# Differential attention's last product with v stationary and two query blocks moving, z_a with channels on the partitions, and the channel sums by a row of ones

## The chip, the cores and the metric

One NeuronCore of a Trainium2 chip runs the whole layer. The metric is the device time of one execution in microseconds (us); lower is better. Engines are named as the profile names them: PE is TensorE, which multiplies matrices (PEld its weight loads), DVE is VectorE, ACT is ScalarE, POOL is GpSimd, and SP is SyncE, which here issues nearly all DMAs (SPq is its queue).

## The reference

One decoder layer on 1024 tokens of width 1024, all in fp32, with two token mixers beside each other:

```
h = RMSNorm(x)
[q | k | v | z_a | xBC | z_s | dt | gate_logits] = h @ w_in
branch A: 8 heads, two softmax maps of head dimension 64 per head, causal:
    a   = softmax(q0 k0^T) - lam * softmax(q1 k1^T)
    o   = a @ v                                  (v has 128 channels per head)
    y_a = rms_norm(o, subln_w) * (1 - lambda_init) * silu(z_a)
branch B: Mamba-2 SSD (32 heads, chunks of 128, state 128) with a causal
    convolution, gated by silu(z_s) and group-normalised -> y_s
merged = sigmoid(g_a) * (y_a @ w_proj_attn) + sigmoid(g_s) * (y_s @ w_proj_ssd)
out    = x + merged @ w_out
```

The change is in branch A: in `a @ v`, in the norm over the 128 channels of a head behind it, and in the projection of z_a.

## The kernel before

The program has no loops on the chip. A planner (class `Plan`) runs while the program is built: every piece of work is a Python generator, and the planner keeps a time `pl.t` for PE and one for each other engine, adds a cost for each instruction, and lets a piece go on when the planned time of what it needs has come. The order in which the instructions are written down is the order of each engine's queue; on the chip each engine follows its queue and waits on semaphores. So the costs in `mm`, `act`, `tt`, `stt` and `load` change no instruction, only the order. Every matmul is recorded on the line of `mm` (L208), every PE transpose on L217, ACT's work on L234, DVE's on L242 or L250, DMAs on L263.

Precision: most products are made of three matmuls of type fp32r (a high and a low part of each operand, `steps3`): `pma<-w,hH` twice and `pma<-w,hL` once per 128 channels of the contraction. Products with plain fp32 operands (`av`, `pO`, `pc`, `pD`, `pacum`, `nwb`) stand in the trace as two MATMUL records each. A name like `pma<-w,hH` reads: output, moving operand, stationary operand.

The stages, in the order of PE's queue:

- The front (the string `FRONT_ORDER`): `y` and `z` steps make z_s, `e` and `g` make part of the gates, `c` the convolved channels of xBC in pairs of blocks, `d` is dt. Chunks of branch B (names `px`, `pS`, `pO`, `pD`, `ab`, `xdt`) run in the gaps from the front on; `PACE` and `SLOW` are the planned distances between them.
- Attention, head by head (`att_proj`): for each of 8 token blocks t, PE multiplies h by the 512 columns of q, k, v and z_a of one head into one PSUM bank `pma`. `att_evac` takes the bank apart: squares for the norm of q and k, a copy of v, `tanh` of the z_a part and (tanh+1)*z_a into `zg` (tokens on the partitions). `qk_stack` transposes q and k (`pq`). `att_block` makes one query block of 128 tokens: scores (`sc`, two maps), exponentials with row sums, the difference of the two maps in `p` (not yet divided by the first map's row sum), then transposes of p in groups of up to four 128x128 blocks (`pa`, copied to `at` by ACT), and then the last product: for each key block j one matmul with at's block stationary and v's block moving, 128 columns wide, into `av` (query tokens on the partitions, channels along the row). Behind it ACT squares `av` with a row sum, POOL makes `f` = (sum + e1)^-0.5 (`rsqrt`, two instructions; e1 holds the epsilon scaled by the softmax's sum), DVE makes y = av * f * zg, PE transposes y (`pya`), ACT copies it to `yt` scaled by subln_w, and four blocks together are stored to `ya_d`.
- The other gates (`pg`), while the last head ends.
- `products`: y_s @ w_proj_ssd and y_a @ w_proj_attn, then `final`: the product with w_out. Sums of w_out's blocks for this are made beforehand by POOL (`weight_sums(2, ...)`, tile `os`), started 11 us after the end of attention's projections in planned time.

PSUM has eight banks, all from one ring (`trs`).

Of the kernel before, what the change touches and what calls it, by code (L numbers as in the profile page):

```python
# [8 lines left out]
F32 = mybir.dt.float32  # L9
# [6 lines left out]
P = 128  # L16
# [129 lines left out]
def tile_hybrid_layer(ctx: ExitStack, tc: tile.TileContext, x, norm_w, w_in, q_norm_w, k_norm_w,  # L146
# [22 lines left out]
    cv_d = dram.tile([3072, S], F32, name="cv_d")  # L169
    z_d = dram.tile([GROUPS, S, 512], F32, name="z_d")  # L170
# [10 lines left out]
    qkm, atm, ytm, smids = Share(mids, 4), Share(mids, 4), Share(mids, 2), Share(mids, 10)  # L181
# [25 lines left out]
    def mm(o, lhsT, rhs, start, stop, after=0.0, **kw):  # L207
        nc.tensor.matmul(o, lhsT=lhsT, rhs=rhs, start=start, stop=stop, **kw)  # L208
# [24 lines left out]
    def act(o, i, f, after, **kw):  # L233
# [5 lines left out]
        return pl.op("A", c, after)  # L239

    def tt(o, a, b, op, after, eng="V"):
# [5 lines left out]
        return pl.op("V", 0.07 + 0.07 * sb + 1.042e-3 * n, after, sb)  # L247

    def stt(o, a, s, b, op0, op1, after):
        nc.vector.scalar_tensor_tensor(out=o, in0=a, scalar=s, in1=b, op0=op0, op1=op1)  # L250
        sb = not in_ps(a, b)
        return pl.op("V", 0.07 + 0.07 * sb + 1.042e-3 * o.free_size() + (0.0 if isinstance(s, float) else 0.06), after, sb)
# [8 lines left out]

    def load(o, i, after=0.0):
        nc.sync.dma_start(out=o, in_=i)  # L263
# [15 lines left out]
    nc.gpsimd.memset(mhalf, -0.5)  # L279
    mone = const.tile([P, 1], F32, name="mone")  # L280
# [511 lines left out]
    def att_proj(h):  # L792
# [5 lines left out]
        zg = bigt([P, NT, P], name=f"zg{h}")  # L798
# [34 lines left out]
    def att_evac(h, t, pm, k, qn, cell):  # L833
        v, zg = hd[h][0:2]
        at = pe_done()
        t2 = act(qn, pm[:, 0:256], AF.Square, at)
        t1 = act(zg[:, t, :], pm[:, 384:512], AF.Tanh, at, scale=0.5)
# [62 lines left out]
    def att_block(h, qb, pk, q):  # L900
# [46 lines left out]
        rec, n0, cc, e1 = tin(1, "rec"), tin(1, "n0"), tin(1, "cc"), tin(1, "e1")  # L947
# [3 lines left out]
        t_e = act(e1, sums[0], AF.Square, at, scale=(P * EPS) ** 0.5)  # L951
# [9 lines left out]
        ats = []  # L961
        for j in range(0, qb + 1, 4):
            w = min(4, qb + 1 - j)
            km = yield from pl.get(atm)
            k = yield from pl.get(trs)
            pt = trt(f"pa{h}{qb}{j}")
            for i in range(w):
                tp(pt[:, i * P:(i + 1) * P], pr[0][:, (j + i) * P:(j + i + 1) * P])
            cell = [midt(name=f"at{h}{qb}{j}"), km]
            pl.spawn(at_evac(pt, k, w, cell), pe_done())  # L970
            ats.append(cell)
        bigs.give(pk[0], pl.t + 0.1)
        for c in ats[:1]:
            while len(c) < 3:
                yield pl.t + 0.1
            yield c[2]
        k = yield from pl.get(trs)
        av = trt(f"av{h}{qb}")
        for j in range(qb + 1):
            c = ats[j // 4]  # L980
# [18 lines left out]
        trs.give(k, at)  # L999
        lefts[h][0] -= 1  # L1000
        if lefts[h][0] == 0:
            for i in ks:
                heads.give(i, at)
        yield at
# [1224 lines left out]
```

## Time and profile before

| | |
|---|---|
| median of 3 runs | 1582.83 us (1580.4 to 1583.64) |
| the profiled execution's own time | 1580.41 us |
| its span in the profile | 1578.7 us |
| mean granted TensorE clock | 0.998 |
| PE, PEld busy share | 98%, 82% |
| DVE, ACT, POOL busy share | 75%, 60%, 50% |
| DMA queue q1, share of 16 engines | 55.7% |

The profile's page has one execution. "Busy" for PE counts from a matmul's start to its modelled end, and neighbouring matmuls overlap, so PE's 98% says that it hardly ever stands without work, and not how long one matmul holds it; that is read from the distance between starts. The stage limits used below are read from the first and last start of the stages' tiles: the front ends and attention begins at 581 us (first `pma`), the last `pya` is at 1275 us, and the rest is products and the final product, to 1579 us.

### The profile page before, as it was taken

What the parts mean: (1) busy time and instruction counts of PE and PEld (TensorE: products, weight loads), DVE (VectorE), ACT (ScalarE), POOL (GpSimd) and SP (SyncE); (2) the same over time, 40 slices, a digit from 0 to 9 for tenths busy, and PEclk for the clock granted to TensorE, in tenths of its full rate; (3) what the DMA queues carried; (4) which work ended last, traced back from release to release, by engine and by line L of the source; (5) the groups of instructions that cost most, each with busy time, mean ns of one, the idle gap of its engine ahead of it and who ended that gap; (6) DMA issues with size and microseconds to landing.
All of it is one profiled execution on the core that took longest, in us unless ns stands there. A gap on an engine that the chain in (4) does not pass through costs nothing.

```text
span 1578.7 us, 24834 instructions
## 1 busy us (share of the span) xinstructions
PE 1553.7 (98%) x7858; PEld 1299.0 (82%) x7858; DVE 1183.6 (75%) x2143; ACT 939.4 (60%) x2273; POOL 785.3 (50%) x906
## 2 busy tenths in 40 slices
PE   7999999999999999999999999999999999999999
PEld 5777888888888888888888888888888888888887
DVE  6778867568787778767778787877556687898985
ACT  7653434467565576778677777776666554443350
POOL 3274465345555554546574846454756745332005
PEclk9999999999999999999999999999999999999999
DMA  6576698744454552424373522333336697798846
GB/s 227 162 250 194 230 301 284 247 153 139 133 150 157 151 158 96 134 62 122 111 236 122 152 89 81 110 112 118 107 134 224 193 366 253 267 323 273 302 140 220
DMA packets 254821, 287.38 MB, mean 182 GB/s; under 512 B 18391, under 2 KB 162528, under 8 KB 254690
## 3 DMA queue, kind: packets, MB, share of 16 engines
q1 hardware_dynamic: 254686, 285.79, 55.7%
q8 instruction: 62, 1.02, 0.3%
q14 instruction: 69, 0.57, 0.1%
q10 hardware_dynamic: 4, 0.00, 0.0%
HBM read 196.47 MB, written 89.26 MB: 181 GB/s over the span
## 4 chain that ended last, share of the span: by engine, by line
PE 85%; ACT 3%; DVE 3%; DMA 3%; POOL 3%; issue 2%; SPq 0%; POOLq 0%; DVEq 0%; ACTq 0%
PE pma L208 19%; PE pz L208 11%; PE py L208 5%; PE fYc L208 5%; PE sc L208 4%; PE pO L208 4%; PE av L208 4%; PE fXc L208 3%; PE fZc L208 3%; PE px L208 3%; PE fYg L208 3%; PE pg L208 2%; PE pmz L208 2%; PE pa L217 2%; PE poz L208 1%
## 5 line engine op out<-in xcount | busy, mean ns | idle before, releaser
L208 PE MATMUL pma<-w,hH 128*128 128x512 f32 x1024 | 343.8, 404 | 0.0
L208 PEld LDWEIGHTS pma<-w,hH 128*128 128x128 f32 x1024 | 187.7, 189 | 32.9 <-DVE xdt L242 0.2
L208 PE MATMUL pma<-w,hL 128*128 128x512 f32 x512 | 205.7, 402 | 0.0
L234 ACT ACTIVATE w<-raw 128x512 fp32r<-128x512 f32 (+1 forms) x166 | 101.3, 629 | 56.0 <-DMA raw<-wf_d 21.7
L242 DVE TENSOR_TENSOR w<-raw,w 128x512 fp32r<-128x512 f32 (+1 forms) x134 | 107.1, 817 | 27.0 <-ACT w L234 24.1
L234 ACT ACTIVATE p<-p,nm 128x256 f32<-128x256 f32 (+7 forms) x128 | 98.8, 774 | 33.8 <-DVE nm L916 33.3
L208 PEld LDWEIGHTS pma<-w,hL 128*128 128x128 f32 x512 | 96.5, 188 | 16.6
L242 POOL TENSOR_TENSOR rawf<-rawf,rawf 128x512 f32<-128x512 f32 x54 | 71.8, 1330 | 75.1 <-DVE wp L242 30.5
L208 PE MATMUL fYc<-ft,wp 128*128 128x512 f32 x432 | 106.5, 392 | 2.4 <-DVE ft L242 1.8
L208 PEld LDWEIGHTS fYc<-ft,wp 128*128 128x128 f32 x432 | 80.3, 188 | 20.2 <-DVE ft L242 2.2
L208 PE MATMUL pz<-w,ft 128*128 128x512 f32 x384 | 90.1, 391 | 0.9 <-DVE w L242 0.9
L234 ACT ACTIVATE wp<-rawp 128x512 fp32r<-128x512 f32 x72 | 44.1, 627 | 78.4 <-POOL rawp L242 25.6
L242 POOL TENSOR_TENSOR os<-os,os 128x512 f32<-128x512 f32 x48 | 66.9, 1393 | 36.4 <-DMA os<-in_w_in_dram 14.8
L208 PEld LDWEIGHTS pz<-w,ft 128*128 128x128 f32 x384 | 71.7, 188 | 16.0 <-DVE w L242 1.3
L242 POOL TENSOR_TENSOR rawp<-rawp,rawp 128x512 f32<-128x512 f32 x36 | 54.4, 1521 | 54.2 <-DVE wp L242 50.2
L234 ACT ACTIVATE ab<-ab,nac 128x128 f32<-128x128 f32 x256 | 78.5, 397 | 3.5 <-POOL ab L1482 3.4
L916 DVE CUSTOM_DVE_ANT_0 p<-sc,maskb 128x512 f32<-128x512 f32 (+3 forms) x128 | 72.4, 584 | 6.6 <-PE sc L208 6.0
L274 POOL TENSOR_TENSOR rs<-rs,mhalf 128x4 f32<-128x4 f32 (+1 forms) x71 | 72.8, 1025 | 5.9
L208 PE MATMUL av<-v,at 128*128 128x128 f32 x576 | 75.2, 275 | 0.0
L208 PEld LDWEIGHTS av<-v,at 128*128 128x128 f32 x576 | 72.5, 191 | 3.2
L234 ACT ACTIVATE wp<-rawf 128x512 fp32r<-128x512 f32 x100 | 60.5, 624 | 17.5 <-POOL rawf L242 16.3
L948 POOL TENSOR_TENSOR rec<-s,mone 128x1 f32<-128x1 f32 x64 | 37.2, 583 | 63.7 <-ACT p L234 62.5
(376 smaller groups left out, 4410.3 us busy)
## 6 DMA issues: line engine op xcount, KB each, us to landing
raw<-in_w_in_dram SPq DMA_DIRECT2D x104, 256.0 KB, 3.2
rawf<-in_w_in_dram SPq DMA_DIRECT2D x72, 256.0 KB, 4.7
ab<-act_d SPq DMA_DIRECT2D x32, 512.0 KB, 4.7
wf_d<-os SPq DMA_DIRECT2D x48, 256.0 KB, 5.1
cv_d<-cv SPq DMA_DIRECT2D x48, 256.0 KB, 2.9
raw<-wf_d SPq DMA_DIRECT2D x48, 256.0 KB, 3.3
t_d<-ts SPq DMA_DIRECT2D x24, 512.0 KB, 4.0
os<-in_w_in_dram SPq DMA_DIRECT2D x32, 256.0 KB, 3.8
```

Source lines behind the costliest of these rows:

```text
L208: nc.tensor.matmul(o, lhsT=lhsT, rhs=rhs, start=start, stop=stop, **kw)
L217: nc.tensor.transpose(out=o, in_=i, identity=ident if idn is None else idn)
L234: nc.scalar.activation(o, i, f, **kw)
L242: (nc.vector if eng == "V" else nc.gpsimd).tensor_tensor(out=o, in0=a, in1=b, op=op)
L274: nc.gpsimd.tensor_tensor(out=dst, in0=dst, in1=mhalf[:, 0:cols], op=ALU.pow)
L916: nc.vector.tensor_tensor_reduce(out=p[:, j:e], in0=sc[i][:, 0:e - j], in1=maskb[:, S - n + j:S - n + e], scale=-1.0, scalar=nms[i - 1] if ...
L948: nc.gpsimd.tensor_tensor(out=rec, in0=sums[1], in1=mone, op=ALU.pow)
```

## The change

The last product is turned. Query blocks are taken in pairs (`att_pair`): p of both blocks is transposed, with the transposes laid out so that for each key block the two query blocks stand side by side in `at` (256 columns). v's block is now the stationary operand and the 256 columns move, so `av` has the 128 channels on the partitions and 256 query tokens along the row. For the last key block of a pair only the second query block is there (128 columns, causal). A head has four pairs; pair i has 2i+1 matmuls of 256 columns and one of 128.

The norm needs a sum over channels, which now lie on the partitions: ACT squares av into `sq`, and one fp32 matmul with a column of ones (`onec`) as the stationary operand and the 256 columns of `sq` moving gives one row of sums in the free half of the same PSUM bank. ACT copies the row, SP stores it in DRAM (`ss_d`). For each half head (`att_norm`) SP loads the sums back with tokens on the partitions (`c4`), POOL makes f for four query blocks at once, SP stores it (`f_d`) and loads it back as a row repeated on all partitions (`fb`), POOL multiplies yt by it, and SP stores yt. DVE makes yt = av * subln_w * zg directly; the transposes `pya` and their copies are gone. z_a is projected with its weights stationary and 512 tokens of h moving (`pga`, two per head, "n0" beside token blocks 0 and 1 and "n1" behind block 7), so zg has channels on the partitions; `pma` is 384 columns wide.

The planner's costs are changed too: an fp32 matmul of n columns was max(4n/2400, 0.215) us and is 2*max(n/2400 + 0.0135, 0.112); DVE's and DMA's costs, the distances of branch B's chunks, the front's order, which weight splits go to POOL, and the planned start of w_out's sums are others.

```
-PACE = 19.5
+PACE = 22.5
-SLOW = 32.0
-FRONT_ORDER = "y0 e6 y1 e0 e4 c6 e2 d0 c20 z06 c16 z07 z05 g0 c2 z04 c0 z16 z03 g2 z17 z15 z14 c4 z13 c8 g8 c14 g6 c22 g10 c12 g4 c10 c18"
+SLOW = 24.0
+FRONT_ORDER = "y0 e0 y1 e6 e2 e4 c20 c18 c6 z06 d0 z07 z05 g0 c16 g4 g2 c2 c0 z03 z16 c4 z17 z15 z14 z13 z04 c22 c14 g8 c8 c10 g6 c12 g10"
-ZSUMS = (75.0, 182.0, 11.0)
-WPOOL = 3
-NEARLY = 48
+ZSUMS = (75.0, 182.0, 1173.0)
+WPOOL = 4
+DMA_PACE = 1.2
+DMA_HOP = 2.0
+NEARLY = 54
...
         if rhs.dtype == F32:
-            c = max(4 * n / 2400, 0.215)
+            c = 2 * max(n / 2400 + lag[0], 0.112)
...
-        zg = bigt([P, NT, P], name=f"zg{h}")
+        zg = bigt([P, S], name=f"zg{h}")
...
-        for ts in ((0, 1), (2,), (3,), (4,), (5,), (6,), (7,)):
+        for ts in ((0, 1, "n0"), (2,), (3,), (4,), (5,), (6,), (7,), ("n1",)):
...
-                    yield from steps3(pm, hblk(kb, t), wide(ids[kb]), kb == 0, kb == KB - 1)
...
+                    if t in range(NT):
+                        yield from steps3(pm[:, 0:384], hblk(kb, t), [x[:, 0:384] for x in wide(ids[kb])], kb == 0, kb == KB - 1)
...
+                    else:
+                        sl = slice(int(t[1]) * 512, int(t[1]) * 512 + 512)
+                        yield from steps3(pm, (w[:, 0, 3, :], w[:, 1, 3, :]), (hH[:, kb, sl], hL[:, kb, sl]), kb == 0, kb == KB - 1)
...
+    def zg_evac(h, sl, pm, k):
+        zg = hd[h][1]
+        at = act(zg[:, sl], pm, AF.Tanh, pe_done(), scale=0.5)
+        yield at
+        at = stt(zg[:, sl], zg[:, sl], 1.0, pm, ALU.add, ALU.mult, at)
+        trs.give(k, at)
...
-            mm(av[:, 0:P], c[0][:, (j % 4) * P:(j % 4 + 1) * P], v[:, j, :], j == 0, j == qb)
...
+            mm(av[:, 0:256], v[:, 2 * g - 2, :], c[0][:, 0:256], g == 1, last, skip_group_check=True)
+            if last:
+                mm(av[:, P:256], v[:, 2 * g - 1, :], c[0][:, 256:384], False, True, skip_group_check=True)
+            else:
+                mm(av[:, 0:256], v[:, 2 * g - 1, :], c[0][:, 256:512], False, False, skip_group_check=True)
...
-        at = act(y, av[:, 0:P], AF.Square, at, accum_out=ss)
-        yield at
-        f = tin(1, "f")
-        at = rsqrt(f, ss, e1, max(at, t_e))
-        yield at
-        at = stt(y, av[:, 0:P], f, zg[:, qb, :], ALU.mult, ALU.mult, at)
...
-        tp(py[:, 0:P], y)
...
-        at = act(yt[0][:, (qb % 4) * P:(qb % 4 + 1) * P], py[:, 0:P], AF.Copy, at, scale=sub_c)
...
+        t1 = act(sq[:, 0:256], av[:, 0:256], AF.Square, at)
...
+        t2 = stt(yt[0][:, i % 2 * 256:i % 2 * 256 + 256], av[:, 0:256], sub_c, zg[:, cs], ALU.mult, ALU.mult, max(at, pl.t))
+        yield max(t1, t2)
+        mm(av[0:1, 256:512], onec, sq[:, 0:256], True, True, skip_group_check=True)
...
+        at = act(sq[0:1, 256:512], av[0:1, 256:512], AF.Copy, at)
...
+        at = load(ss_d[h:h + 1, cs], sq[0:1, 256:512], at)
...
+    def att_norm(h, half, yt):
...
+        at = load(c4, ss_d[h, sl].rearrange("(b q) -> q b", q=P), pl.t)
+        yield at
+        at = rsqrt(f4, c4, e1, max(at, *e_at))
+        yield at
+        at = load(f_d[h, sl].rearrange("(b q) -> q b", q=P), f4, at)
...
+        at = load(fb, f_d[h, sl].partition_broadcast(P), pl.t)
+        yield at
+        at = tt(yt[0], yt[0], fb, ALU.mult, max([at] + yt[2]), "G")
...
+        at = load(ya_d[h * P:(h + 1) * P, sl], yt[0], at)
...
-        pl.spawn(weight_sums(2, w_o, 0, pl.t + ZSUMS[2]))
```

How the change moves instructions is shown at three places. A row is one instruction of the queue, with its tile numbers; "x2" means two in a row.

PE's queue at the start of head 3 (`pma30` is head 3, token block 0; w108 are its weights for the first 128 channels of the contraction). Before:

```order
L208 MATMUL pma30_8552<-w108_7531,hH_114 128x512 x2
L208 MATMUL pma30_8552<-w108_7531,hL_115 128x512
L208 MATMUL pma31_8554<-w108_7531,hH_114 128x512 x2
L208 MATMUL pma31_8554<-w108_7531,hL_115 128x512
L208 MATMUL pma30_8552<-w109_8466,hH_114 128x512 x2
```

After (`pga3n0` is z_a of head 3 for tokens 0 to 511; `pO24` is branch B's):

```order
L213 MATMUL pma30_8606<-w108_7699,hH_118 128x384 x2
L213 MATMUL pO24_8615<-sh23_8274,ch24_8549 128x512
L213 MATMUL pO24_8615<-sl23_8275,ch24_8549 128x512
L213 MATMUL pO24_8615<-sh23_8274,cT24_8333 128x512
L213 MATMUL pma30_8606<-w108_7699,hL_119 128x384
L213 MATMUL pma31_8608<-w108_7699,hH_118 128x384 x2
L213 MATMUL pma31_8608<-w108_7699,hL_119 128x384
L213 MATMUL pga3n0_8609<-hH_118,w108_7699 128x512
L213 MATMUL pga3n0_8609<-hL_119,w108_7699 128x512
L213 MATMUL pga3n0_8609<-hH_118,w108_7699 128x512
```

The z_a columns have left `pma` and come as three matmuls of their own, with h moving, behind the two token blocks.

PE's queue where a head's last query block is multiplied with v. Before, head 3, blocks 6 and 7 (`av36`; `pya35` is the transpose of block 5's y):

```order
L217 MATMUL pq401_10433<-ident_99,qk40_9784 128x128 x2
L217 MATMUL pq401_10433<-ident_99,qk42_9959 128x128 x2
L217 MATMUL pya35_10438<-ident_99,y35_10337 128x128
L208 MATMUL av36_10440<-v3_8548,at360_10390 128x128 x4
L208 MATMUL av36_10440<-v3_8548,at364_10403 128x128 x3
L217 MATMUL pa370_10449<-ident_99,p370_10275 128x128 x4
L217 MATMUL pa374_10455<-ident_99,p370_10275 128x128 x4
L208 MATMUL pma45_10428<-w116_8670,hH_114 128x512
L208 MATMUL pma45_10428<-w116_8670,hL_115 128x512
L208 MATMUL pma45_10428<-w117_9664,hH_114 128x512 x2
```

After, the last pair of head 2 (`av23`) and the first pair of head 3 (`av30`; `sc33...` are scores of head 3; `at23x` are the transposed blocks):

```order
L213 MATMUL av23_9531<-at232_9539,v2_7616 128x256 x2
L213 MATMUL av23_9531<-at233_9546,v2_7616 128x256
L213 MATMUL av23_9531<-at233_9546,v2_7616 128x128
L213 MATMUL pga3n1_9592<-hH_118,w108_7699 128x512
L213 MATMUL sc3300_9597<-kk30_8604,qh30_9247 128x512
L213 MATMUL sc3300_9597<-kk30_8604,qlo0_5752 128x512
L213 MATMUL av30_9600<-at300_9561,v3_8602 128x256
L213 MATMUL av30_9600<-at300_9561,v3_8602 128x128
L213 MATMUL sc3310_9606<-kk31_8605,qh30_9247 128x512
L213 MATMUL sc3310_9606<-kk31_8605,qlo0_5752 128x512
L213 MATMUL pga3n1_9592<-hL_119,w108_7699 128x512
L213 MATMUL av23_9531<-sq23_9594,onec_99 1x256
```

Matmuls of 128 columns, one per key block and query block, have become matmuls of 256, one per key block and pair. The transpose of y is gone, and the row of sums (`av23<-sq23,onec`, 1x256) stands eight matmuls behind the product that it waits for, through ACT's square.

SP's queue around the store of a half head's result. Before (head 0, second half; the other rows are branch B's loads and next weights):

```order
L263 DMA xr17_7206<-cv_d_89 128x4x128
L263 DMA bT17_7208<-cv_d_89 128x128
L263 DMA cT17_7209<-cv_d_89 128x128
L263 DMA zc16_7238<-z_d_90 128x512
L263 DMA ab17_7290<-act_d_87 128x1024
L263 DMA ya_d_84<-yt04_6865 128x512
```

After (head 0, second half: the row of sums, the sums back by tokens, f out, f back as rows):

```order
L281 DMA ss_d_90<-sq03_7148 1x256
L281 DMA ts000_7209<-ys_d_85 128x1024
L281 DMA ts001_7210<-ys_d_85 128x1024
L281 DMA c4_7213<-ss_d_90 128x4x1
L281 DMA t_d_93<-ts000_7209 128x1024
L281 DMA zc20_7368<-z_d_92 128x512
L281 DMA f_d_91<-f4_7214 128x4x1
L281 DMA t_d_93<-ts001_7210 128x1024
L281 DMA fb01_7425<-f_d_91 128x512
```

One store has become the end of a chain of transfers (two `ss_d`, `c4`, `f_d`, `fb`, then the store), and the loads of branch B stand between them in the same queue.

More of the change, by code (lines that the diff above doesn't have):

```diff
@@ L246, in tt @@
         sb = not in_ps(a, b)
-        return pl.op("V", 0.07 + 0.07 * sb + 1.042e-3 * n, after, sb)
+        return pl.op("V", 0.065 + part(o) + 1.042e-3 * n, after, sb)
     def stt(o, a, s, b, op0, op1, after):
@@ L960, in att_block, with att_pair @@
         yield at
[L961 to L980, printed above, removed]
+        pair = tails.setdefault((h, qb // 2), {})
+        pair[qb % 2] = (pr[0], pk[0], at)
+        if len(pair) == 2:
+            yield from att_pair(h, qb // 2, tails.pop((h, qb // 2)), ks)
+    e4s, tails = {}, {}
+    def att_pair(h, i, pair, ks):
+        v, zg = hd[h][0:2]
+        ps = [pair[x][0] for x in range(2)]
+        n, half = i + 1, i // 2
+        cells = []
+        kv = None
+        for g in range(n + 1):
+            if g < n:
+                km = yield from pl.get(atm)
+                k = yield from pl.get(trs)
+                pt = trt(f"pa{h}{i}{g}")
+                blocks = [(2 * g, 0), (2 * g, 1), (2 * g + 1, 0), (2 * g + 1, 1)] if g < n - 1 else [(2 * g, 0), (2 * g, 1), (2 * g + 1, 1)]
+                for b, (j, x) in enumerate(blocks):
+                    tp(pt[:, b * P:(b + 1) * P], ps[x][:, j * P:(j + 1) * P])
+                cells.append([midt(name=f"at{h}{i}{g}"), km])
+                pl.spawn(at_evac(pt, k, len(blocks), cells[g]), pe_done())
+                if g == n - 1:
+                    for x in range(2):
+                        bigs.give(pair[x][1], pl.t + 0.1)
+            if g == 0:
+                continue
+            c = cells[g - 1]
             while len(c) < 3:
@@ L984, in att_block @@
                 yield c[2]
-            mm(av[:, 0:P], c[0][:, (j % 4) * P:(j % 4 + 1) * P], v[:, j, :], j == 0, j == qb)
-        for c in ats:
+            if kv is None:
+                kv = yield from pl.get(trs)
+                av = trt(f"av{h}{i}")
+            last = g == n
+            mm(av[:, 0:256], v[:, 2 * g - 2, :], c[0][:, 0:256], g == 1, last, skip_group_check=True)
[3 more added lines that the diff above has]
+                mm(av[:, 0:256], v[:, 2 * g - 1, :], c[0][:, 256:512], False, False, skip_group_check=True)
@@ L1001, in att_block @@
[L1001 to L1004, printed above, removed]
+        cs = slice(i * 256, i * 256 + 256)
+        sq = midt(name=f"sq{h}{i}")
+        t1 = act(sq[:, 0:256], av[:, 0:256], AF.Square, at)
         yts = lefts[h][1]
-        if qb // 4 not in yts:
+        if half not in yts:
             km = yield from pl.get(ytm)
-            if qb // 4 not in yts:
-                yts[qb // 4] = [midt(name=f"yt{h}{qb}"), km, 0]
+            if half not in yts:
+                yts[half] = [midt(name=f"yt{h}{half}"), km, []]
@@ L1019, in att_block @@
-        at = act(yt[0][:, (qb % 4) * P:(qb % 4 + 1) * P], py[:, 0:P], AF.Copy, at, scale=sub_c)
-        trs.give(k, at)
-        yt[2] += 1
-        if yt[2] == 4:
-            yield at
-            at = load(ya_d[h * P:(h + 1) * P, qb // 4 * 512:qb // 4 * 512 + 512], yt[0], at)
-            ytm.give(yt[1], at)
-            ready.setdefault("att", []).append(at)
+        at = act(sq[0:1, 256:512], av[0:1, 256:512], AF.Copy, at)
+        trs.give(kv, max(at, t2))
+        lefts[h][0] -= 2
+        if lefts[h][0] == 0:
+            for q in ks:
+                heads.give(q, max(at, t2))
```

96 lines of the change are left out of this document (64 added, 32 removed).

## The prediction

> **What bounds the kernel now.** I read the page's busy shares and clock first, then the busy time of each engine by stage, the waits of PE, and the chain that ended last.
>
> ```profile
> PE 1553.7 (98%) x7858; PEld 1299.0 (82%) x7858; DVE 1183.6 (75%) x2143; ACT 939.4 (60%) x2273; POOL 785.3 (50%) x906
> ...
> PEclk9999999999999999999999999999999999999999
> ...
> PE 85%; ACT 3%; DVE 3%; DMA 3%; POOL 3%; issue 2%; SPq 0%; POOLq 0%; DVEq 0%; ACTq 0%
> ```
>
> ```profile
> 0.00:20.00 20.00, 14.23 (x44) 9.03 (x45) 10.44 (x18) 13.32 (x24) 4.20 (x16) 1.00 0.84 288
> 20.00:581.00 561.00, 548.86 (x2547) 450.26 (x2546) 417.05 (x651) 312.75 (x607) 284.98 (x241) 1.00 0.60 193
> 581.00:1276.00 695.00, 692.86 (x3950) 593.74 (x3949) 507.77 (x1110) 491.48 (x1430) 400.85 (x586) 1.00 0.42 135
> 1276.00:1579.00 303.00, 297.71 (x1321) 245.93 (x1319) 248.34 (x366) 121.84 (x215) 95.32 (x64) 1.00 0.78 263
> ```
>
> The columns of the second are length, then busy us of PE, PEld, DVE, ACT and POOL, the clock, the DMA share and GB/s. In attention (581 to 1276 us) PE lacks work for 695 - 692.86 = 2.1 us, while DVE, ACT and POOL are busy 73%, 71% and 58% of the stage. The clock is full. So PE's queue sets the end, and the change is worth what it does to the time that PE's instructions hold PE. Idle PE time lies in the front (561 - 548.86 = 12.1 us), at the start and at the end. What ended it in the front and in attention, longest first:
>
> ```profile
> PE pmz L208 <- ACT zc L234: 2.9, 1, 2.9
> PE pe L208 <- ACT gc L234: 2.9, 4, 0.7
> PE fYc L208 <- DVE ft L242: 1.8, 1, 1.8
> ...
> PE pa L217 <- DVE p L250: 0.4, 1, 0.4
> PE pya L217 <- DVE xdt L242: 0.4, 1, 0.4
> PE pya L217 <- ACT yt L234: 0.3, 1, 0.3
> ```
>
> **What one matmul holds PE.** Mean durations overlap, so I take steps between starts from the timeline (start, length of the row, operation, count).
>
> ```profile
> 144.72 1.52 PE L208 MATMUL pz<-w,ft 128*128 128x512 f32 x6
> 146.08 0.59 PE L208 MATMUL pacum<-tv,tri 128*128 128x256 f32 x2
> 146.51 0.59 PE L208 MATMUL pacum<-tv,ones 128*128 128x256 f32 x2
> ...
> 626.51 0.34 PE L208 MATMUL sc<-kk,qh 128*128 128x384 f32 x1
> 626.68 0.34 PE L208 MATMUL sc<-kk,qlo 128*128 128x384 f32 x1
> ...
> 1572.23 1.24 PE L208 MATMUL pod<-w,mt 128*128 128x256 f32 x9
> ...
> 714.79 1.95 PE L208 MATMUL av<-v,at 128*128 128x128 f32 x16
> ...
> 1264.87 1.04 PE L217 MATMUL pa<-ident,p 128*128 128x128 f32 x8
> ```
>
> - fp32r, 512 columns: six take 1.52, the last one's own length is 0.39 (mean of such rows), so (1.52 - 0.39) / 5 = 0.226.
> - fp32r, 256 columns: (1.24 - 0.28) / 8 = 0.12. So 256 columns more cost 0.106, and a matmul has some 0.014 that its columns don't explain.
> - fp32r, 384 columns: half-way between, 0.173; the two `sc` rows start 626.68 - 626.51 = 0.17 apart.
> - fp32, 128 columns (av as it is): (1.95 - 0.27) / 15 = 0.112 a record, two records a product: 0.224.
> - fp32, 256 columns: only `pacum` has them. 146.51 - 146.08 = 0.43 for one product of two records.
> - transposes: (1.04 - 0.27) / 7 = 0.11.
>
> The 0.43 decides the case. Twice the columns cost twice the time: 256 columns hold PE for 0.43 and two times 128 for 0.448. The planner of the changed kernel counts 2*(256/2400 + 0.0135) = 0.24 for the same product. The Trainium skill, page "FP8 and Floating Point Precision", section "TensorE Precision Notes", says that true fp32 takes four passes through the array; four times 256 columns at the 2.4 GHz of its page "TensorE: Matmul & The Clock Gate" would be 0.427, and the two rows of `pacum` agree with it.
>
> **The change part by part, on PE.**
>
> 1. `av`, turned. Before, 8 heads x 36 blocks = 288 products (576 records) x 0.224 = 64.5 us. After, per head 1+3+5+7 = 16 of 256 columns and 4 of 128: 128 x 0.43 + 32 x 0.224 = 55.0 + 7.2 = 62.2. Gain 2.3.
> 2. Channel sums, new: 32 products of 256 columns. That only one column is stationary does not help:
>
> ```profile
> L208 PE MATMUL pdt<-hH,w 128*64 128x512 f32 x16 | 6.1, 390 | 0.0
> L208 PE MATMUL pdt<-hL,w 128*32 128x512 f32 x16 | 6.0, 395 | 0.0
> ```
>
> With 32 stationary columns a matmul lasts as long as with 64 (0.395, 0.390) and as long as the 0.39 of 128; the moving side sets it. 32 x 0.43 = 13.8 us.
> 3. `pya`, gone: 64 x 0.11 = 7.0 us gained.
> 4. z_a apart. Before 1536 matmuls of 512 columns: 1536 x 0.2265 = 347.9. After 1536 x 0.173 + 384 x 0.2265 = 265.7 + 87.0 = 352.7. As many columns, 384 instructions more: 4.8 us lost. The skill's page "TensorE: Matmul & The Clock Gate", section "Wait — 56ns, not 53.3ns?", gives a fixed 2.5 ns per matmul above its columns; by that this term would be 384 x 0.0025 = 1.0 and the sum 3.8 lower. The rows show 14 ns, so I keep 4.8.
>
> Sum on PE: -2.3 + 13.8 - 7.0 + 4.8 = +9.3 us.
>
> **What lies beside it.**
>
> ```profile
> L234 ACT ACTIVATE y<-av x64: 258/277/323, 638.0 to 1269.5; 128x128 f32<-128x128 f32 x64
> L234 ACT ACTIVATION_READ_ACCUMULATOR y<-av x64: 193/195/258, 638.1 to 1269.6; 128x1 f32 x64
> L250 DVE SCALAR_TENSOR_TENSOR y<-av,f,zg x64: 333/345/352, 642.6 to 1272.5; 128x128 f32<-128x128 f32 x64
> ...
> L234 ACT ACTIVATE yt<-pya,cols x64: 347/367/404, 645.9 to 1276.1; 128x128 f32<-128x128 f32 x64
> ...
> L273 POOL TENSOR_TENSOR f<-ssv,e x64: 181/190/1004, 638.6 to 1270.7; 128x1 f32<-128x1 f32 x64
> L274 POOL TENSOR_TENSOR f<-f,mhalf x64: 537/542/1600, 638.9 to 1271.4; 128x1 f32<-128x1 f32 x64
> ...
> L234 ACT ACTIVATE qk<-pma x64: 359/383/421, 592.7 to 1206.7; 128x256 f32<-128x256 f32 x64
> ...
> L242 POOL TENSOR_TENSOR os<-os,os x48: 1272/1296/2081, 87.8 to 1290.8; 128x512 f32<-128x512 f32 x48
> ```
>
> ACT loses 64 x (0.277 + 0.195 + 0.367) = 53.7 us and gets 32 squares and at most as long row copies, 64 x 0.383 = 24.5. POOL loses 64 x (0.190 + 0.542) = 46.8 and gets 16 multiplications of 128x512, 20.7, and 16 times f for four blocks. DVE does 32 wider products for 64. None of these engines bounds the stage, so I cost this at 0; without PE's queue as cover it would be a gain. SP gets 80 small DMAs more, of which `c4` and `f_d` move single fp32 numbers, and the order shows loads of branch B standing behind `c4` and `fb`. No row has such a transfer; the nearest, `ya_d<-yt`, lands in 2.4 us and the slowest often used in 5.7. Five in series are 12 to 29 us from sum to store. Who needs y_a:
>
> ```profile
> L263 SPq DMA_DIRECT2D ts<-ya_d x8: 319/380/546, 1050.5 to 1311.6; - x8
> ```
>
> The last of it is loaded at 1311.6, 37 us after the last `pya` (1275), so even the last head's chain is in time: 0, and at most some us if SP's queue holds weights up.
>
> **A new wait.** The row of sums stands in PE's queue and needs ACT's square. What that takes, at a place where ACT was free:
>
> ```profile
> 1268.36 1.05 PE L208 MATMUL av<-v,at 128*128 128x128 f32 x8
> ...
> 1269.45 0.28 ACT L234 ACTIVATE y<-av 128x128 f32<-128x128 f32 x1 [1.34 <-PE av L208]
> ...
> L234 ACT ACTIVATE p<-p,nm 128x256 f32<-128x256 f32 (+7 forms) x128 | 98.8, 774 | 33.8 <-DVE nm L916 33.3
> ```
>
> The last av record ends at 1269.41, 0.16 behind its columns; ACT starts 0.04 later, and a square of 256 columns takes 0.383: 0.58 us and a handover. At the place shown of the order, eight matmuls stand between (pga, four sc, av30's two, pga: 6 x 0.226 + 0.43 + 0.224 = 2.0 us), at the tightest some 0.8. So the cover holds where ACT is free and is gone where an exponential of 0.774 is ahead of the square. Behind a waiting PE everything queues, and the next exponentials' scores come late. Bounds: 0.7 in all, what `pya` waits today, and 32 x 0.774 = 24.8. Most places have more than 1.3 us of cover, so I take 2, near the lower end.
>
> **The front.** The same steps in another order, and no row shows the new one. It can at most give back its 12.1 us of idle PE, and might as well double them; four of the waits (2.9 us) belong to the `e` steps, which are all still there. I take 0, with -8 to +8 as likely ends. Moving w_out's sums ahead takes POOL and DMA work out of the crowded 35 us behind attention, where PE lacked 5.3 us up to the end in all: 0, at most -2.
>
> Sum: 9.3 + 2 = 11.3 on the profiled execution's own 1580.4 (1.7 around its span) gives 1591.7. That execution was 2.4 below the median of the three runs, so against that median the same kernel would read 1594.
>
> **The rivals.**
>
> - Faster: the wide move runs at the planner's price, 0.24 a product. 160 products x (0.43 - 0.24) = 30.4 less: 1561. It stops being slower where a product costs under 0.43 - 11.3/160 = 0.36. For it: `pO` moves 64 columns and is no cheaper than av's 128 (a mean of 272 against 275 ns), so 0.112 may be a floor and not the columns. Against: both pacum rows. 7%.
> - No change: front and end give back about 10 of their idle us. 1582, anything from 1577 to 1583.6. 15%. With no new wait and nearly all idle time gone it could be just faster, 2%.
> - Slower still: PE waits for ACT at half of the sums for one exponential (12.4) or the longer hold of PSUM banks and the new front cost as much: 1599 to 1615, say 1604. For it: the lead of the sums is a third of that of `pya` today. Against: PE takes longer than planned at each wide product, so the others come early. 14%.
> - As summed, 1584 to 1599: 62%.
>
> ```profile
> L208 PE MATMUL pO<-xdt,ab 128*128 128x64 f32 x448 | 53.2, 272 | 1.4 <-POOL wp L242 1.4
> L208 PE MATMUL av<-v,at 128*128 128x128 f32 x576 | 75.2, 275 | 0.0
> ```
>
> **How the numbers follow.** 1592 is the likeliest case. The range leaves out the 7% and 2% below and some 9% of the slowest: 1578 to 1603. About 0.2% (3.2 us) is what a measurement of this kernel can tell from no change. Faster by that: 0.07 + 0.02 + 0.01 of the front's case; the same: the rest of that case and the lowest part of the summed one, 0.16; slower: 0.74.
>
> **What would show it.** In the profile after, rows of `av` with 128x256 starting 0.43 apart per product (0.24 would be the first rival); 32 rows of `1x256`-wide sums of the same step; no `pya`; `pma` at 0.173 a matmul; attention from first `pma` to last sum longer by about 10 us with PE's idle time in it still under 5 us; the waits of PE `av` for ACT `sq` near 2 us in total; the front's idle time within 4 to 20 us. I am wrong if the front's end moves by more than 8 us, or if the 256-column step is not what `pacum` shows.

## The result, and the profile after

The changed kernel takes 1664.28 us (median of 5 runs, 1661.53 to 1667.49) against 1582.83 (5 runs, 1580.4 to 1584.17): ratio 1.0517 [1.0498, 1.0536]. It is 5% slower; 1592 was predicted, with 1603 as the upper end. The profiled execution took 1665.63 us, its span is 1663.9.

The page's busy shares, clock and packet counts, and the busy time by stage (length, PE, PEld, DVE, ACT, POOL, clock, DMA share, GB/s; attention is now 600 to 1341 us):

```profile
PE 1597.1 (96%) x7986; PEld 1356.1 (82%) x7986; DVE 1157.4 (70%) x2072; ACT 929.1 (56%) x2085; POOL 762.9 (46%) x818
...
DMA packets 274084, 291.68 MB, mean 175 GB/s; under 512 B 35575, under 2 KB 179744, under 8 KB 273954
```

```profile
0.00:20.00 20.00, 14.80 (x49) 9.46 (x50) 11.58 (x19) 14.78 (x25) 5.02 (x19) 1.00 0.82 285
20.00:600.00 580.00, 561.37 (x2595) 459.05 (x2594) 426.13 (x692) 331.83 (x645) 286.39 (x244) 0.99 0.61 191
600.00:1341.00 741.00, 704.32 (x3951) 626.16 (x3949) 469.58 (x988) 451.70 (x1184) 361.60 (x484) 0.97 0.44 122
1341.00:1663.00 322.00, 316.59 (x1396) 261.44 (x1395) 250.16 (x376) 130.80 (x232) 109.94 (x72) 0.99 0.81 263
```

In attention PE now lacks work for 741 - 704.32 = 36.7 us instead of 2.1, and the granted clock has fallen to 0.97, which over 741 us is at most another 22 (a part of it falls on time in which PE stands anyway). The stage also moved fewer bytes per second (122 against 135 GB/s), so this is no lack of bandwidth. Packets under 512 bytes rose from 18391 to 35575.

To compare kernels I took each kind of matmul's own step (the steps of the prediction), times its count in a stage, off the stage's length. What is left is the time in which PE waited or ran at a lowered clock. Here the start runs from the first matmul to 100 us, the front from there to the first `pma`, and "behind" ends with the last matmul:

| | PE's own steps | start | front | attention | behind |
|---|---|---|---|---|---|
| before | 1530.0 | 16.6 | 11.4 | 11.9 | 2.5 |
| after | 1539.8 | 18.1 | 21.6 | 72.5 | 5.7 |

So of 85.2 us between the two profiled executions, 9.8 are PE's own steps (9.3 predicted), 60.6 are attention's waits, 10.2 the front's.

**One episode.** The store `f_d<-f` (four fp32 numbers of each of 128 partitions, 512 pieces of 4 bytes in DRAM) was at first only a suspect; this is what stands around one of its 16 issues. First SP's queue in the timeline, then PE's, then busy time in steps of 2 us:

```profile
873.70 0.37 SPq L281 DMA_DIRECT2D f_d<-f  x1
874.17 0.46 SPq L281 DMA_DIRECT2D xr<-cv_d  x1
...
883.03 0.32 SPq L281 DMA_DIRECT2D fb<-f_d  x1
```

```profile
879.50 0.34 PE L213 MATMUL pma<-w,hL 128*128 128x384 f32 x1
885.82 1.08 PE L222 MATMUL px<-ident,xr 128*128 128x128 f32 x4 [5.98 <-DMA xr<-cv_d]
```

```profile
874.00:876.00 2.00, 1.91 (x13) 1.61 (x12) 1.95 (x6) 2.00 (x9) 0.00 (x0) 1.00 0.16 9
876.00:878.00 2.00, 2.00 (x14) 1.91 (x13) 2.00 (x4) 2.00 (x7) 1.27 (x2) 1.00 0.09 1
878.00:880.00 2.00, 1.84 (x11) 1.52 (x9) 1.85 (x6) 0.20 (x2) 0.00 (x0) 1.00 0.30 49
880.00:882.00 2.00, 0.00 (x0) 0.00 (x0) 1.09 (x3) 0.00 (x0) 0.00 (x0) 1.00 0.25 29
882.00:884.00 2.00, 0.00 (x0) 0.00 (x0) 0.00 (x0) 0.00 (x0) 0.80 (x2) 0.65 0.11 20
884.00:886.00 2.00, 0.18 (x1) 0.21 (x2) 0.42 (x1) 0.00 (x0) 0.46 (x1) 0.50 0.64 154
886.00:888.00 2.00, 2.00 (x10) 2.00 (x10) 0.00 (x0) 1.05 (x2) 0.00 (x0) 0.50 1.01 317
...
892.00:894.00 2.00, 2.00 (x10) 1.86 (x9) 1.85 (x6) 1.00 (x2) 0.07 (x1) 0.79 0.36 133
```

The store is issued at 873.70, and `fb`, which waits for it, at 883.03: 9.3 us. For most of that time the DMA engines move 1 to 49 GB/s, although three loads of branch B are queued. Their first, `xr`, is needed by PE's `px`, which stands still from 879.8 to 885.8 with everything behind it. (The DMA share in these steps is 0.09 to 0.30: the DMA engines are on record as idle for most of them.) POOL stands too:

```profile
876.46 1.04 POOL L298 TENSOR_TENSOR rs<-rs,mhalf 128x4 f32<-128x4 f32 x1
883.12 0.23 POOL L295 TENSOR_SCALAR rs<-ss 128x4 f32<-128x4 f32 x1 [5.61 <-DMA f_d<-f]
883.43 1.03 POOL L298 TENSOR_TENSOR rs<-rs,mhalf 128x4 f32<-128x4 f32 x1
888.01 1.27 POOL L250 TENSOR_TENSOR yt<-yt,fb 128x512 f32<-128x512 f32 x1 [3.55 <-DMA fb<-f_d]
```

The norm of q and k (`rs`) sits in POOL's queue, first behind a tile buffer that the store still reads, elsewhere behind the product with `fb`; DVE's `qk` and the next scores need it. The third cost is in the clock column: PE's first idle 2 us are still at 1.00, then it is granted 0.65 and 0.50 and has full speed again only after 892. In this trace the grant is either 1.00 or 0.50, so 0.65 in the step from 882 puts the fall at 882.6 and 0.79 in the step from 892 the return at 892.8. Half speed begins 2.8 us after PE stops, and the first 7 us of work after the 6 us of waiting run at it. By the Trainium skill, page "TensorE: Matmul & The Clock Gate", section "What's actually happening", the clock is halved after an idle window of about 3.4 us and restored after as long a busy one, and these windows run on freely. The trace agrees in kind, but here the return took twice such a window of work.

The waits as the profile adds them up (us in total, times, longest), of SP's queue and then of the engines:

```profile
SPq L281 <- DMA f_d<-f: 111.0, 15, 9.8
```

```profile
POOL yt L250 <- DMA fb<-f_d: 79.4, 14, 10.5
...
PE px L222 <- DMA xr<-cv_d: 16.1, 6, 6.0
POOL rs L295 <- DMA f_d<-f: 15.9, 3, 7.1
...
PE pa L222 <- ACT at L239: 4.8, 1, 4.8
...
PE sc L213 <- DVE qk L250: 4.6, 1, 4.6
...
PE pq L222 <- DVE qk L250: 3.2, 1, 3.2
...
PE av L213 <- ACT at L239: 2.3, 1, 2.3
...
PE sc L213 <- ACT sq L239: 1.2, 1, 1.2
```

Of PE's 36.7 idle us in attention 16.1 end with the late `xr`. The 4.6 before `sc` come through POOL's queue:

```profile
982.30 0.23 POOL L295 TENSOR_SCALAR rs<-ss 128x4 f32<-128x4 f32 x1 [7.07 <-DMA f_d<-f]
983.69 0.42 DVE L250 TENSOR_TENSOR qk<-pma,rs 128x256 f32<-128x256 f32 x1 [4.57 <-POOL rs L298]
984.17 0.79 PE L213 MATMUL sc<-kk,qh 128*128 128x512 f32 x1 [4.61 <-DVE qk L250]
```

So do the 3.2 before `pq` (POOL stood 7.5 us for `fb` just before) and the 2.3 before `av` (ACT's `at` waited 4.2 for POOL's product with `fb`): 10.1 in all. The 4.8 before `pa` come through SP's queue, which stood until it could issue `fb`, with four loads of weights behind it, and through ACT's queue, where the copy `at` stood behind the first of these weights:

```profile
846.82 0.33 SPq L281 DMA_DIRECT2D fb<-f_d  x1
847.26 2.08 SPq L281 DMA_DIRECT2D raw<-in_w_in_dram  x4
```

```profile
852.20 0.63 ACT L239 ACTIVATE w<-raw 128x512 fp32r<-128x512 f32 x1 [5.74 <-DMA raw<-in_w_in_dram]
...
853.00 0.59 ACT L239 ACTIVATE at<-pa 128x512 f32<-128x512 f32 x1
```

### The profile page after: what moved, and what is told of

It is laid out like the page before. It is cut to its first block, busy times and chain, and to the rows that moved or that the text cites. A ratio compares the mean times of both kernels' runs of the same rounds, so it can differ in the third digit from the quotient of the medians.

```text
span 1663.9 us, 24851 instructions
## 1 busy us (share of the span) xinstructions
PE 1597.1 (96%) x7986; PEld 1356.1 (82%) x7986; DVE 1157.4 (70%) x2072; ACT 929.1 (56%) x2085; POOL 762.9 (46%) x818
## 5 line engine op out<-in xcount | busy, mean ns | idle before, releaser
L213 PE MATMUL pma<-w,hH 128*128 128x384 f32 x1024 | 282.9, 348 | 0.0
L213 PEld LDWEIGHTS pma<-w,hH 128*128 128x128 f32 x1024 | 187.3, 191 | 11.8 <-issue 4.4
L213 PE MATMUL pma<-w,hL 128*128 128x384 f32 x512 | 177.6, 347 | 0.0
L239 ACT ACTIVATE w<-raw 128x512 fp32r<-128x512 f32 x166 | 100.9, 624 | 61.8 <-DMA raw<-in_w_in_dram 17.6
L250 DVE TENSOR_TENSOR w<-raw,w 128x512 fp32r<-128x512 f32 x143 | 106.3, 761 | 29.2 <-ACT w L239 27.4
L952 DVE CUSTOM_DVE_ANT_0 p<-sc,maskb 128x512 f32<-128x512 f32 (+3 forms) x128 | 72.5, 586 | 13.9 <-PE sc L213 13.4
L213 PE MATMUL av<-at,v 128*128 128x256 f32 (+1 forms) x320 | 76.8, 371 | 2.4 <-ACT at L239 2.3
L295 POOL TENSOR_SCALAR rs<-ss 128x4 f32<-128x4 f32 (+1 forms) x71 | 20.8, 292 | 120.7 <-DVE ss L878 85.6
L213 PE MATMUL sc<-kk,qh 128*128 128x512 f32 (+3 forms) x192 | 69.0, 365 | 6.1 <-DVE qk L250 4.6
```

Of the source, the lines that this page charges most:

```text
L239: nc.scalar.activation(o, i, f, **kw)
L250: (nc.vector if eng == "V" else nc.gpsimd).tensor_tensor(out=o, in0=a, in1=b, op=op)
L295: nc.gpsimd.tensor_scalar(out=dst, in0=src, scalar1=add, scalar2=None, op0=ALU.add)
L952: nc.vector.tensor_tensor_reduce(out=p[:, j:e], in0=sc[i][:, 0:e - j], in1=maskb[:, S - n + j:S - n + e], scale=-1.0, scalar=nms[i - 1] if ...
```

## The experiments

The suspects were the scattered store with the chain behind it, the new order of the queues (front numbers and planner costs), and the changed arithmetic itself. Ratios are to the kernel before, with its 95% interval; "waits" is the table's measure by start, front, attention, behind.

**Store in 16-byte pieces (e1).** In after:

```
-        at = load(f_d[h, sl].rearrange("(b q) -> q b", q=P), f4, at)
+        at = load(f_d[h, sl].rearrange("(q b) -> q b", b=4), f4, at)
```

> The changed kernel with one edit: the factor f of four query blocks is stored as 128 pieces of 16 bytes, and not as 512 single numbers of 4 bytes (the numbers then come back in another order, so the result is not the reference's). Theory A, the scattered store: in the trace of the changed kernel f_d lands 9.2 us after its issue (873.7 to 882.9), SP stands 111 us behind it and POOL 79 us behind fb. If its length goes with the number of pieces, it lands in 2 to 3 us, SP's wait for f_d falls below 35 us, and the time falls from 1664 to 1600 to 1620. Theory B, the planner's price of the wide product (0.24 for 0.43) or the new order of the front: nothing of that is touched, 1655 to 1670.

Measured: 1624.71 us, 1.0271 [1.0246, 1.0295]; waits 18.8, 21.2, 29.6, 9.5. As many bytes from the same tile, 128 pieces instead of 512: 39.6 us of the 81.5 are gone, all from attention (72.5 to 29.6). That is 5 us short of what theory A expected. The windows around one such store, issued at 680.5 (`fb` 2.4 us later), show a dip of one step instead of four:

```profile
680.00:682.00 2.00, 2.00 (x13) 1.83 (x12) 1.85 (x9) 1.37 (x5) 1.19 (x3) 1.00 0.57 138
682.00:684.00 2.00, 2.00 (x10) 1.65 (x9) 0.50 (x4) 1.31 (x4) 0.70 (x2) 1.00 0.07 8
684.00:686.00 2.00, 2.00 (x12) 1.82 (x12) 2.00 (x4) 0.60 (x1) 0.04 (x1) 1.00 0.82 141
```

**Front's numbers of before under the new costs (e2).** In after, `FRONT_ORDER`, `PACE`, `SLOW`, `WPOOL` and `NEARLY` of before.

> The changed kernel with the front's order, the distances of branch B's chunks and the numbers for POOL's weight splits (FRONT_ORDER, PACE, SLOW, WPOOL, NEARLY) as before. PE's idle time from 100 to 581 us is 12.8 in the trace after and 7.2 before, so theory A (scattered store) says 1650 to 1664: at most the front's 6 us and a little come back. Theory C, the new order and pace cause the loss: 1595 to 1610.

Measured: 1690.56, 1.0696 [1.0676, 1.0716]; waits 14.8, 25.7, 100.1, 6.1. That is above both expected ranges: under the new costs before's front numbers don't give the short front back (25.7), and attention gets worse by 28.

**The wide matmul planned at its true price (e3).** In after:

```
-            c = 2 * max(n / 2400 + lag[0], 0.112)
+            c = 2 * max(2 * n / 2400, 0.112)
```

> The changed kernel with the planner's price of an fp32 matmul at what the trace shows (0.43 for 256 columns, 0.224 for 128), which only moves instructions. Theory B, the under-priced wide products put the work of the other engines too late for PE: 1600 to 1630. Theory A: the stall of 9 us at each store stays as it is, 1650 to 1670.

Measured: 1675.32, 1.0597 [1.058, 1.0614]; waits 17.5, 19.7, 86.4, 6.0. That is also above both ranges. Planned at the true price the kernel gets slower, so that the planner takes half of what the chip takes is not the cause.

**The store alone, added to before (e4).** Sixteen stores of a constant, which nobody reads, one behind each `ya_d`:

```
+            load(f_d[h, qb // 4 * 512:qb // 4 * 512 + 512].rearrange("(b q) -> q b", q=P), mhalf, at)
```

> The kernel before with 16 stores added, one behind each half head's result: a constant of 128x4 numbers is scattered to DRAM as 512 single numbers, and nobody reads it. Theory A in its strong form (the store blocks the DMA rings for all behind it): each store lands in 9 us, loads issued right behind it land late by as much, and the time rises by 10 to 40 us to 1590 to 1625. If only the chain f_d, fb, POOL matters (those who wait for the store itself), 1583 to 1586.

Measured: 1639.34, 1.0356 [1.032, 1.0393]; waits 13.7, 12.5, 70.7, 4.9. No arithmetic, no order numbers and no reader, and attention's waits reach what they are in after. 58 us for 16 stores is 3.6 each; 10 to 40 in all were expected.

**Sums and f without DRAM (e5).** In after, `sq` is stationary and the column of ones moves, so the sums come with tokens on the partitions; f is spread over the partitions by four PE transposes of a repeated column, and DVE multiplies from PSUM. The transfers `ss_d`, `c4`, `f_d` and `fb` are gone:

```
-        mm(av[0:1, 256:512], onec, sq[:, 0:256], True, True, skip_group_check=True)
+        for b in range(2):
+            mm(av[:, 256 + b:257 + b], sq[:, b * P:(b + 1) * P], onec, True, True, skip_group_check=True)
...
-        at = load(f_d[h, sl].rearrange("(b q) -> q b", q=P), f4, at)
...
+        for b in range(4):
+            tp(fb[:, b * P:(b + 1) * P], f4[:, b:b + 1].to_broadcast([P, P]))
+        at = tt(yt[0], yt[0], fb, ALU.mult, max([pe_done()] + yt[2]))
```

> The changed kernel without its four transfers: the sums are taken with sq stationary and the column of ones moving, so that they come out by tokens (two fp32 products of one column per pair, 0.224 each, for one of 0.43), and f is spread over the partitions by four PE transposes of a repeated column, which DVE multiplies with yt from PSUM. PE work: 64 transposes x 0.11 = 7 us more than the changed kernel. If the transfers are all of the attention's loss: 1664 less the 50 us of PE waits and slow clock there plus 7, about 1615 to 1625, the same as with 16-byte pieces (1625) or a little under. If waits of PE for ACT's squares or the wide product's price carry a share, it stays above 1635.

Measured: 1614.91, 1.0206 [1.0184, 1.0228]; waits 17.5, 22.0, 14.6, 6.8. Its attention (window 599 to 1293):

```profile
599.00:1293.00 694.00, 690.14 (x4092) 635.31 (x4090) 485.20 (x1003) 445.32 (x1186) 348.05 (x475) 1.00 0.41 128
```

The turned product itself runs attention in 694 us with 3.9 of idle PE at full clock, as before's did in 695 with 2.1. Of after's waits in attention 57.9 us (72.5 less 14.6) went with the detour through DRAM. Even so this kernel is 33 us slower than before: by the steps PE's own work is some 17 us more than before's (after's 9.8, and 64 x 0.11 for the transposes), and the rest are waits, 10.6 of them in the front.

**No chain at all (e6).** In after, `ss_d`, `c4`, f, `f_d`, `fb` and the product with them are left out; the row of sums is still made and copied.

> The changed kernel with the norm's chain left out: the row of sums is still made and copied, but neither stored nor used, yt is stored as it is. What is left against the kernel before is PE's own work (9 us), the squares and sums, the front and the planner's numbers. If the remaining 43 us of the version with 16-byte pieces lie in the chain (SP and POOL waiting in order), 1590 to 1600; if they lie in the front, the order and the planner's costs, 1615 to 1625.

Measured: 1619.19, 1.0235 [1.0217, 1.0254]; waits 16.2, 22.0, 23.7, 10.7. Attention's waits are then 11.8 above before's, so the row of sums with its wait for ACT can have at most that much of the 60.6.

**The planner of after alone (e7), its costs alone (e9), its numbers alone (e10).** Before's attention, with the new cost lines in `mm`, `act`, `tt`, `stt`, `load` and the new numbers (e7), with the cost lines only (e9), with `FRONT_ORDER`, `PACE`, `SLOW`, `ZSUMS`, `WPOOL`, `NEARLY` only (e10).

> The kernel before with all of the planner's numbers of the changed one (costs of mm, act, tt, stt and load, FRONT_ORDER, PACE, SLOW, ZSUMS, WPOOL, NEARLY) and the attention as before. In the trace after, the front's idle time (20 to 581 us) is some 7 us above that of before and the stage behind attention has waits of 5 us that it had not. If those come from the new numbers: 1590 to 1605. If they come from the new attention: 1578 to 1586.

> The kernel before with the planner's costs alone of the changed one (mm, act, tt, stt, load), its own front order and paces. All planner numbers together made it 20 us slower (1602 against 1581.5). If the new costs put work too late for PE: 1595 to 1610. If the new front order and paces are the cause: 1578 to 1586.

> The kernel before with the front's order and the other numbers alone (FRONT_ORDER, PACE, SLOW, ZSUMS, WPOOL, NEARLY), the planner's costs as before. In the trace with all planner numbers the front's PE idle time is 18.7 us against 12.1, with waits at fXg (3.5), fYg (3.1) and pS (2.2) that before has not. If the order makes them: 1590 to 1605. If the costs do: 1578 to 1586.

Measured: 1602.06, 1.0123 [1.0098, 1.0149]; 1605.2, 1.015 [1.0133, 1.0167]; 1606.66, 1.0161 [1.0146, 1.0176]. Fronts 23.4, 24.1, 27.0 instead of 11.4, attention 19.1, 19.1, 18.8 instead of 11.9. Either half costs all of it, and both together no more: the either-or of the three expectations doesn't hold.

**f stored as four rows of 512 bytes (e8).** In after, PE transposes f (one matmul), ACT copies the four rows, and SP stores them:

```
-        at = load(f_d[h, sl].rearrange("(b q) -> q b", q=P), f4, at)
+        tp(pf[0:4, 0:P], f4)
...
+        at = act(fr[0:4], pf[0:4, 0:P], AF.Copy, at)
...
+        at = load(f_d[h, sl].rearrange("(b q) -> b q", q=P), fr[0:4], at)
```

> The changed kernel with f transposed by PE (16 transposes of four columns, under 2 us) and copied by ACT, so that it is stored as 4 rows of 512 bytes and not as 512 numbers; all else as in the changed kernel. The same cure as 16-byte pieces with the right result: f_d lands in 2 to 3 us and the time is 1612 to 1628. If it is the chain's length and not the pieces, the two more steps make it no faster than 1650.

Measured: 1634.17, 1.0334 [1.0317, 1.0351]; waits 18.5, 21.9, 24.8, 21.2. Attention is healed as in e1 and e6; the whole is slower than expected by what came behind it. The 21.2 behind it hold one wait of 16.0 us of `pz` for DVE's `px`, which no other run has; why is open.

**After's attention with before's planner, with the chain (e11) and with e5's sums (e12).** All costs and numbers of before.

> The changed attention alone: all planner costs and numbers as before. If the parts add up, the time is 1581.5 plus PE's 9.5, plus the 45 us between the changed kernel (1664) and the one without the norm's chain (1619), plus some 8 left over there: 1636 to 1648. If new attention and new numbers belong together (the order was chosen for it), it is slower than the changed kernel: over 1664.

> The changed attention without its four transfers (sums by tokens, f spread by PE), with all planner costs and numbers as before. PE's own work is 9.5 + 7 us more than before. If nothing else is lost: 1595 to 1602, the fastest of the turned ones and still slower than before. If order and attention belong together: 1612 or more.

Measured: 1680.59, 1.0653 [1.0607, 1.0699], waits 15.7, 11.4, 75.7, 30.5; and 1611.71, 1.0197 [1.0182, 1.0213], waits 15.6, 15.4, 22.0, 5.7. With before's planner the front is 11.4 again in e11 (15.4 in e12), so the front's 10 us are the planner's. But against after e11 loses 16 us, and against e5 e12 gains 3: what the front gives, attention or the end takes. The end of e11 (30.5) wasn't followed further.

**Which property of the store costs (e13, e14, e15).** In before again, at e4's place: the same store from ACT's queue, a store in 16-byte pieces, and a load that gathers 512 single numbers into a tile nobody reads:

```
+            nc.scalar.dma_start(out=f_d[h, qb // 4 * 512:qb // 4 * 512 + 512].rearrange("(b q) -> q b", q=P), in_=mhalf)
```

```
+            load(f_d[h, qb // 4 * 512:qb // 4 * 512 + 512].rearrange("(q b) -> q b", b=4), mhalf, at)
```

```
+            load(tiny.tile([P, 4], F32, tag="g4", name="g4", bufs=4), conv_w[0, h % 4, qb // 4 * 512:qb // 4 * 512 + 512].rearrange("(b q) -> q b", q=P), at)
```

> The kernel before with the 16 added scattered stores (512 numbers of 4 bytes each) issued from ACT's queue and not from SP's, where the added stores cost 58 us (1639). If the store holds up only what stands behind it in its own queue: 1581 to 1590, and the other transfers go on beside it. If it holds the DMA engines or the way to DRAM themselves: 1615 to 1645, and the bytes moved per us fall for 8 to 9 us behind each store as they do from SP.

> The kernel before with 16 added stores of the same 2 KB each, as 128 pieces of 16 bytes, issued from SP. Theory A (the number of pieces sets the time): each takes 2 to 3 us, 1581 to 1595. If any small store of this kind holds the queues, or the added instruction alone shifts the order: 1620 to 1645.

> The kernel before with 16 added loads in place of the stores: 512 numbers of 4 bytes gathered from DRAM into a tile that nobody reads. The changed kernel's c4 is such a load. If small reads hold the queues as small writes do: 1615 to 1645; if it is only the writes: 1581 to 1592.

Measured: 1641.91, 1.0393 [1.0372, 1.0415]; 1590.05, 1.0062 [1.0045, 1.0078]; 1588.36, 1.0056 [1.004, 1.0072]. Attention's waits 68.0, 19.0, 19.0. So it is neither SP's queue nor the number of pieces by itself: from ACT's queue the store costs as much (62 us against 58, on before medians 1.4 apart), and 512 pieces read cost no more than 128 pieces written, 9 to 10 us over 16 transfers, with the same 19 us of attention's waits as in e7, e9 and e10, whose orders are shifted too. Some 10 of e4's 58 us are thus what any such transfer costs at this place, and some 48 (3.0 a store) what the pieces of 4 bytes add. Whether for a store it is their number or their size isn't separated: e14 has a quarter as many, each four times as long. Windows of e13 around a store issued by ACT at 850.4, then of e14 (831.6) and e15 (830.9):

```profile
850.00:852.00 2.00, 2.00 (x12) 1.69 (x11) 1.94 (x5) 2.00 (x9) 1.92 (x3) 1.00 0.13 1
852.00:854.00 2.00, 2.00 (x12) 1.70 (x11) 1.85 (x8) 1.68 (x7) 2.00 (x2) 1.00 2.05 262
854.00:856.00 2.00, 2.00 (x14) 1.69 (x13) 1.85 (x7) 2.00 (x7) 1.75 (x4) 1.00 0.26 8
856.00:858.00 2.00, 2.00 (x12) 1.72 (x11) 1.83 (x7) 1.93 (x7) 1.83 (x3) 1.00 1.69 51
858.00:860.00 2.00, 2.00 (x11) 1.66 (x11) 1.85 (x8) 1.48 (x5) 0.76 (x3) 1.00 0.25 16
860.00:862.00 2.00, 2.00 (x11) 1.65 (x10) 1.88 (x4) 1.30 (x7) 1.09 (x4) 1.00 0.75 210
```

```profile
833.00:835.00 2.00, 2.00 (x11) 1.65 (x10) 1.92 (x4) 2.00 (x10) 1.05 (x1) 1.00 0.99 337
```

```profile
832.00:834.00 2.00, 2.00 (x11) 1.62 (x10) 1.96 (x4) 2.00 (x10) 1.29 (x1) 1.00 0.90 299
```

In e13 the step from 852 holds one burst, and the other four up to 860 have 1 to 51 GB/s, with the store in ACT's queue (SP has issued branch B's loads from 856.6 on); some 2 us behind the issues of e14's store and e15's load traffic is at 337 and 299 GB/s. (Where the DMA share is above 1, packets are counted whole in one step.)

## Why the prediction was wrong

Right in direction, and wrong by 72 us.

**The step that failed** is in "What lies beside it": five small transfers in series, "12 to 29 us from sum to store", cost 0, "and at most some us if SP's queue holds weights up". The price and the question were both wrong.
- The price. It was taken from `ya_d<-yt`, whose 2.4 us belong to whole rows, with the note that no row has a transfer of single numbers. `f_d` takes about 9 (9.3 in the episode). By the Trainium skill, page "DMA: Bandwidth & Descriptors", section "Rules for kernel authors", a last dimension with a stride becomes one descriptor (one piece of the transfer) per element; the count agrees, since 2 x 16 x 512 = 16384 of the 17184 new packets under 512 bytes are those of `c4` and `f_d`. That rule holds for `c4` as for `f_d`, and e15 shows the reading kind to be nearly free, so the number of pieces alone didn't give the cost either.
- The question. I asked who needs y_a, and found it 37 us late enough. It should have been who else uses the DMA engines meanwhile. The path is: `f_d` holds traffic, `xr` comes late, PE waits at `px`, the clock is lowered; beside it POOL waits in order for `fb` or for the buffer, and `qk` waits for POOL; and SP's queue, which the prediction gave "at most some us", stood 111 us for `f_d`, with weights behind it. e4 puts the store into before (58 us); e1, e5, e6 and e8 take it out of after (30 to 49 us of the total, 43 to 58 of attention's waits). Of PE's 36.7 idle us in after, 20.9 end with late loads (`xr`, and the 4.8 behind the weights) and 10.1 through POOL, as the profile names the releasers; how the lowered clock divides between them isn't separated. In e4 and e13 no instruction reads what is stored, so there held traffic is enough.

**The front: 0, "-8 to +8 as likely ends".** PE's idle time in it went from 12.1 to 580 - 561.37 = 18.6 us, inside the forecast 4 to 20, but with the clock's 0.99 the waits grew by 10.2 (from 100 us on), and its end moved by 18 (6.4 of it work of PE that was done later before, 11.7 waits from the start on), which the prediction named as its failure from 8 on. e7, e9 and e10 have it without the new attention, e11 hasn't with before's planner. That each of these three other orders costs before 20 to 26 us, and that the parts don't add, is shown; why, wait by wait, is not settled. The end, forecast at 0 to -2, has 3.2 us more of waits; the part of w_out's sums in that isn't isolated.

**What held.** PE's own steps: +9.8 against +9.3. PE's timeline, with a pair of `pma` rows, a pair of query blocks (three products of 256 columns and one of 128, eight records) and a row of sums:

```profile
599.54 0.51 PE L213 MATMUL pma<-w,hH 128*128 128x384 f32 x2
599.88 0.34 PE L213 MATMUL pma<-w,hL 128*128 128x384 f32 x1
...
664.58 1.68 PE L213 MATMUL av<-at,v 128*128 128x256 f32 x8
...
708.42 0.59 PE L213 MATMUL av<-sq,onec 128*1 128x256 f32 x2
```

`pma` steps by (599.88 - 599.54) / 2 = 0.17 (0.173 forecast). The pair's eight starts lie 1.68 - 0.27 = 1.41 apart, the last record's own length off; six records at 0.215 and one at 0.112 make 1.40, so a wide product holds PE for the forecast 0.43. The row of sums is 0.59 - 0.38 = 0.21 between its two starts, the same with one stationary column. The rival "faster", by which the wide move costs 0.24, is out. The new wait (2 forecast, for PE behind ACT's square) is at most 0.8 in front of the rows of sums, by the last column of the group below, and 0.5 of that ended with DVE's `yt`; 1.2 came once where `sc` stands behind a square, as shown above. The rival "slower still" named other causes: PE's waits for ACT at the sums, which didn't come, and PSUM banks; 1664 is also beyond its 1599 to 1615.

```profile
L213 PE MATMUL av<-sq,onec 128*1 128x256 f32 x64 | 18.8, 377 | 0.8 <-DVE yt L258 0.5
```

## What to carry to other kernels

Sixteen stores of 2 KB cost the kernel before 58 us in pieces of 4 bytes and 10 in pieces of 16, and sixteen loads in pieces of 4 bytes cost 9. So before calling a small DMA hidden, look how it is cut at its DRAM end and in which direction it goes, and look for a row with the same pieces; where there is none, the price is open, and the bound is what every other load then queued would lose. Off the critical path isn't free on a shared resource: ask who else uses the DMA engines while it runs, and what stands behind the waiting instruction in each in-order queue. And a new order isn't free either: three other orders of the same work (e7, e9, e10) each cost before 20 to 26 us.

## What the runs showed of the hardware

- A store of 512 separate 4-byte pieces to DRAM takes about 9 us and holds nearly all other DMA traffic for most of that time (1 to 51 GB/s in most steps), whichever of SP's and ACT's queues issues it. 2 KB in 16-byte pieces took 2.4 us from its issue to its reader's; 512 4-byte pieces read left traffic at 299 GB/s within 2 us. In after's trace the packets of the store issued at 873.70 are on record for 9 ns or less each and have all begun within 1.3 us of the issue, so most of the 9.3 us to its reader lies behind them. The Trainium skill's page "DMA: Bandwidth & Descriptors", section "Specifications", says that a transfer below 512 bytes becomes a read-modify-write; the pieces of both stores are below that, so the rule alone doesn't tell 9 us from 2.4, and which part of a write takes the time isn't shown.
- A wait of PE can cost more than its length: 6 us of idle time were followed by 7 us of work at a granted clock of 0.50. Over attention the clock's 0.97 is at most 22 us beside 36.7 us of idle time.
